# Handing the residual scaling out between feed-forward tiles and pointwise products, with no weight parts made ahead at three layer norms

## The chip, the cores and the metric

One core of a Trainium2 chip runs the whole kernel in one launch. The metric is the time of the execution on the device in microseconds; the median of several runs is what counts. The core's engines are TensorE (PE, matrix products; PEld is its loading of stationary tiles), VectorE (DVE), ScalarE (ACT) and GpSimd (POOL); the load queue on SyncE (SP) starts almost all transfers. Each engine takes its instructions strictly in order, so an instruction that waits holds up all that stand behind it on the same engine.

## The reference

Two layers of a diffusion trunk work on 256 latent and 256 context tokens of width 1024. A layer has a mixing half (attention, a convolution branch and a pooling branch, merged by gates and projected by `w_out`) and a feed-forward half. Each half ends in a residual sum and a layer norm; the context tokens are carried through the first layer only. Cut to what matters here:

```python
for l in range(DEPTH):
    ml = ada_mod(c, w_ada[l], b_ada[l], N_MOD)[:, None]
    mc = ada_mod(c_ctx, w_ada[l], b_ada[l], 2 if last else N_MOD)
    hl = modulate(x, ml[..., 0, :], ml[..., 1, :])
    ...
    x = layer_norm(DEEPNORM_ALPHA * x + ml[..., 2, :] * mix(zl, attn_l), ln1_g[l], ln1_b[l])
    x = layer_norm(DEEPNORM_ALPHA * x + ml[..., 5, :] * ffn(modulate(x, ml[..., 3, :], ml[..., 4, :])),
                   ln2_g[l], ln2_b[l])
    ...                                    # the same for ctx, in the first layer

def conv_ffn(h, w_up, dw_w, dw_b, w_down):
    a, u = jnp.split(h @ w_up, 2, axis=-1)
    a = depthwise_conv(a, dw_w, dw_b)
    return (jax.nn.silu(a) * u) @ w_down
```

So a layer norm's result goes two ways: modulated into the next product, and, scaled by the norm's gain and ALPHA, into the next residual sum. The second use isn't due until that next sum.

## The kernel before

**Products.** A float32 product is made of three: an operand is split into a rounded part hi and a remainder lo (activations into `hh` and `hl`), and PE adds hi·hi, lo·hi and hi·lo (L423, L424, L425). Results lie in four PSUM tiles `mm`; a new product needs a free one, so it waits until DVE or ACT has read the tile before it.

**Weights.** `ORDER` lists all weight chunks (128x1024, 512 KB) in the order of their use. `load_to` issues their loads on SP's queue some chunks ahead of use; chunks land in five `raw` and three `rawt` buffers. `split_to` makes a chunk's hi on ACT (L279) and its lo on DVE (L283); there are five buffers of each. `take` hands a chunk out and splits three chunks further on (L292). `take_ada` (L304) goes through the chunks of the conditioning row ("ada"), which `ada` (L340) multiplies with the conditioning vector; for a gate it adds a bias row `bg`, which is loaded at the fifth of the eight chunks (L344), into `adarow` (L356), and sends the row through DRAM to be broadcast. The layer-1 convolution's weights are split during layer 0's feed-forward half, and of these only hi is made at use.

**Residual.** `evict` multiplies a finished sum with its gate (`tg`, L540), adds the residual tile `x` (L541) and takes the statistics (L544). `norm` makes mean and inverse deviation and normalizes two 128x512 tiles, one on DVE (L559), one on ACT (L560). `modulated` transposes the result in PE (L568) and makes for each of eight slices k `hh` on ACT (L583), a float32 `h` on DVE (L585) and `hl` on DVE (L588). `scaled` multiplies each residual tile with ALPHA and the gain (L595) and adds the bias (L596): two DVE instructions a tile, eight tiles in layer 0 and four in layer 1. The gain and bias rows `prow` are loaded just before (L334).

**The order around a layer norm.** After each norm the first three weight items of the next half run slice by slice over all three (`mm_by_k`), so that PE can start with slice 0. In layer 0's first norm (L1150 to L1158) the second half of the tokens follows; then at L1169 to L1172 the bias is multiplied with ALPHA and the eight tiles are scaled, and only then the feed-forward loop (L1178) begins, which for each of 22 tiles j runs two products `pa` and `pu`, a three-tap convolution over `pa` into `acc` (ACT L1182, DVE L1186 and L1189: the last reader of `pa`), a silu (L1193), the product with `pu` (L1194) and a split for the down product (L1200, L1201). In layer 1 the scaling for the mixing half's sum stands at L1137 to L1141, behind the eight pointwise products `pw` (L1111 to L1123), where the bias of `w_out` times the gate is also joined into the bias row (L1139, L1140).

The kernel is recorded through a layer that orders each engine's instructions by their dependencies and by program order; `pin` and `keep_in_program_order` fix some of them.

## Time and profile before

| | before |
|---|---|
| median of 3 runs | 1432.54 us (1432.14 to 1434.34) |
| the profiled execution | 1433.01 us, of which the span is 1431.2 us |
| mean granted TensorE clock | 0.988 |
| PE, DVE, ACT, POOL busy | 1382.7, 1093.3, 683.0, 66.1 us |
| transfers | 265.22 MB, 185 GB/s in the mean |

A row of a list of instructions reads: start in us from the span's beginning, duration, engine, line, operation, written tile <- read tiles, shape, how many were merged; in brackets the engine's idle time ahead of it and what ended it. The granted clock is TensorE's, as a share of full speed.

The time in layer 0's first norm lies at 530 to 590 us, its second norm at 905 to 946 us; layer 1's pointwise products, `w_out`, and first norm at 1167 to 1245 us.

### The profile page before, as it was taken

What the parts mean: (1) busy time and instruction counts of PE and PEld (TensorE: products, weight loads), DVE (VectorE), ACT (ScalarE), POOL (GpSimd) and SP (SyncE); (2) the same over time, 40 slices, a digit from 0 to 9 for tenths busy, and PEclk for the clock granted to TensorE, in tenths of its full rate; (3) what the DMA queues carried; (4) which work ended last, traced back from release to release, by engine and by line L of the source; (5) the groups of instructions that cost most, each with busy time, mean ns of one, the idle gap of its engine ahead of it and who ended that gap; (6) DMA issues with size and microseconds to landing.
All of it is one profiled execution on the core that took longest, in us unless ns stands there. A gap on an engine that the chain in (4) does not pass through costs nothing.

```text
span 1431.2 us, 20768 instructions
## 1 busy us (share of the span) xinstructions
PE 1382.7 (97%) x7896; PEld 1173.4 (82%) x7896; DVE 1093.3 (76%) x1931; ACT 683.0 (48%) x1088; POOL 66.1 (5%) x65
## 2 busy tenths in 40 slices
PE   7999999999999999899999999899999999799997
PEld 5777778888877888688888888699889998799985
DVE  3598896996994778867666877378899969777745
ACT  3332446555737314445454322253687773455541
POOL 0020320000000000000000000010400000000000
PEclk9999999999999999999999999989999999899999
DMA  9654332223233526476676787588633347755560
GB/s 352 240 186 138 126 99 88 82 97 105 93 118 133 178 73 239 149 271 246 233 244 238 238 321 253 204 308 325 234 115 113 113 166 246 253 189 180 187 211 30
DMA packets 80788, 265.22 MB, mean 185 GB/s; under 512 B 9240, under 2 KB 9904, under 8 KB 80560
## 3 DMA queue, kind: packets, MB, share of 16 engines
q1 hardware_dynamic: 79968, 263.03, 52.8%
q8 instruction: 62, 1.02, 0.3%
q10 hardware_dynamic: 720, 0.87, 0.2%
...
## 4 chain that ended last, share of the span: by engine, by line
PE 88%; DVE 7%; DMA 2%; ACT 1%; issue 1%; POOL 1%; SPq 0%; POOLq 0%; DVEq 0%; ACTq 0%
PE mm L423 26%; PE mm L424 26%; PE mm L425 26%; PE ax L457 3%; DVE lo L283 1%; PE ax L991 1%; PE ad L349 1%; DVE H L780 1%; DMA prow<-in_rows 1%; PE ax L425 1%; PE ax L423 1%; PE ad L671 1%; PE ax L424 1%; DMA bg<-in_bgate 1%; DVE x L596 1%
## 5 line engine op out<-in xcount | busy, mean ns | idle before, releaser
L423 PE MATMUL mm<-hh,hi 128*128 128x256 f32 (+1 forms) x1112 | 354.6, 321 | 14.9 <-DVE acc L1189 9.8
L279 ACT ACTIVATE hi<-raw 128x1024 fp32r<-128x1024 f32 x208 | 215.8, 1046 | 309.4 <-PE mm L424 124.3
L424 PE MATMUL mm<-hl,hi 128*128 128x256 f32 (+1 forms) x1112 | 354.6, 319 | 1.6 <-DVE hl L588 1.6
L425 PE MATMUL mm<-hh,lo 128*128 128x256 f32 (+1 forms) x1112 | 354.4, 319 | 0.0
L283 DVE TENSOR_TENSOR lo<-raw,hi 128x1024 fp32r<-128x1024 f32 (+1 forms) x191 | 229.6, 1204 | 100.5 <-ACT hi L279 96.8
L780 DVE SCALAR_TENSOR_TENSOR H<-gl,vt,H 128x502 f32<-128x502 f32 (+29 forms) x480 | 264.7, 606 | 0.2
L423 PEld LDWEIGHTS mm<-hh,hi 128*128 128x128 f32 x1112 | 215.1, 194 | 30.7 <-issue 12.0
L424 PEld LDWEIGHTS mm<-hl,hi 128*128 128x128 f32 x1112 | 215.6, 194 | 16.2 <-DVE hl L588 2.4
L425 PEld LDWEIGHTS mm<-hh,lo 128*128 128x128 f32 x1112 | 215.5, 194 | 14.9 <-issue 2.0
L423 PE MATMUL mm<-hi,hi 128*128 128x512 f32 x464 | 185.2, 399 | 2.0 <-DVE nat L915 2.0
L425 PE MATMUL mm<-hi,lo 128*128 128x512 f32 x368 | 144.3, 392 | 1.1 <-DVE lo L283 1.1
L424 PE MATMUL mm<-xlo,hi 128*128 128x512 f32 x368 | 144.1, 392 | 0.0
L279 ACT ACTIVATE hi<-rawt 128x1024 fp32r<-128x1024 f32 (+1 forms) x83 | 86.7, 1048 | 108.4 <-PE mm L425 51.4
L283 DVE TENSOR_TENSOR lo<-rawt,hi 128x1024 fp32r<-128x1024 f32 (+1 forms) x72 | 86.5, 1205 | 32.5 <-ACT hi L279 32.5
L423 PEld LDWEIGHTS mm<-hi,hi 128*128 128x128 f32 x464 | 87.3, 188 | 27.7 <-issue 6.0
L423 PE MATMUL mm<-hi,ah 128*128 128x512 f32 x264 | 102.8, 390 | 0.0
L424 PE MATMUL mm<-lo,ah 128*128 128x512 f32 x264 | 102.8, 389 | 0.0
L425 PE MATMUL mm<-hi,al 128*128 128x512 f32 x264 | 102.6, 389 | 0.0
L425 PEld LDWEIGHTS mm<-hi,lo 128*128 128x128 f32 x368 | 69.1, 188 | 16.1 <-DVE lo L283 1.6
L424 PEld LDWEIGHTS mm<-xlo,hi 128*128 128x128 f32 x368 | 69.2, 188 | 13.8 <-issue 0.4
L381 DVE CUSTOM_DVE_ANT_0 prod<-rawt,cb,vt 128x1024 f32<-128x1024 f32 x48 | 61.5, 1282 | 4.2 <-DMA rawt<-in_wst 3.6
L423 PEld LDWEIGHTS mm<-hi,ah 128*128 128x128 f32 x264 | 49.6, 188 | 10.9 <-issue 0.3
...
## 6 DMA issues: line engine op xcount, KB each, us to landing
raw<-in_wst SPq DMA_DIRECT2D x232, 512.0 KB, 4.4
rawt<-in_wst SPq DMA_DIRECT2D x160, 512.0 KB, 4.3
scr<-rawt SPq DMA_DIRECT2D x28, 512.0 KB, 4.7
lo<-scr SPq DMA_DIRECT2D x28, 512.0 KB, 4.4
...
```

Of the source, the lines that this page charges most:

```text
L279: pin(A.activation(hi[:, :w], r[:, :w], AF.Copy))
L283: pin(V.tensor_tensor(lo[:, :w], r[:, :w], hi[:, :w].bitcast(F32), op=ALU.subtract))
L349: PE.matmul(ps[32 * j:32 * j + 32, :], sc[:, k, :], w[:, j * 256:(j + 1) * 256], start=(k == 0), stop=(k == KT - 1),)
L381: tc.keep_in_program_order(V.tensor_tensor_reduce(prod, w, cb[:, s], 1.0, col(l, "b_ada", m * 8 + c), ALU.mult, ALU.add, mods[l, m][:, c, ...
L423: pin(PE.matmul(ps, lh, rh, start=(first and i == 0), stop=False))
L424: pin(PE.matmul(ps, lh, rl, start=False, stop=False))
L425: pin(PE.matmul(ps, ll, rh, start=False, stop=(last and i == n - 1)))
L457: PE.matmul(ps, x[:, a:b], y[:, c:d], start=(i == 0), stop=(i == n - 1))
L596: V.tensor_tensor(x, x, b[h], op=ALU.add)
L671: pin(PE.matmul(ad0_ps[q][32 * j:32 * j + 32, :P], sc[:, k, :], w[:, j * P:(j + 1) * P], start=(k == 0), stop=(k == KT - 1),))
L780: V.scalar_tensor_tensor(h[:, :, a:b], g[:, :, a + d:b + d], col(l, "dw_w", k * 8 + j), h[:, :, a:b], op0=ALU.mult, op1=ALU.add,)
L991: PE.transpose(t_ps[:, kt * 256 + q2 * P:kt * 256 + (q2 + 1) * P], p[:, o:o + P], ID)
```

## The change

Four edits:

1. `scaled` returns a list of closures, one for each residual tile (two DVE instructions each, kept in program order) in place of doing the work. In the feed-forward loop one closure is called in each tile from j = 2 on: first the two multiplications of the bias with ALPHA, then the eight (layer 1: four) tiles.
2. In layer 1 the gate tile and the rows for the mixing half are loaded ahead of the pointwise products; at the fourth of the eight products the two bias rows are joined, and at each of the next four a residual tile is scaled.
3. A list `only` is filled at layer 0's two norms and layer 1's first: while it holds something, `take` splits only the chunk that it hands out, and `take_ada` doesn't split at all. `split_on`, called after `modulated`, ends this and splits the three chunks ahead.
4. A gate's bias row `bg` is loaded ahead of its first ada chunk, in `load_to`.

```diff
--- before.py
+++ after.py
@@ -219,8 +219,10 @@
 
 
     raw, split = {}, {}
+    bias_of = {}
     xr = []
     nxt = {"load": 0, "split": 0, "use": 0}
+    only = []
 
     others = [i for i, it in enumerate(ORDER) if it[0] not in ("ada", "adt", "pre", "ad0", "x")]
     sides = [i for i, it in enumerate(ORDER) if it[0] in ("adt", "pre")]
@@ -247,6 +249,9 @@
                 continue
             if it[0] == "pre":
                 w = CH
+            if it[0] == "ada" and it[3] == 0 and it[1:3] in GATES:
+                bias_of[it[1:3]] = S(name="bg")
+                load(bias_of[it[1:3]][:, :256], bgate[GATES.index(it[1:3])], False)
 
             if it[0] in ("adt", "pre") or (not side(nxt["load"]) and nxt["load"] % (NRAW + NRAWT) >= NRAW):
                 t = wp.tile([P, CH], F32, tag="rawt", name=f"rawt{nxt['load']}", bufs=NRAWT)
@@ -289,7 +294,7 @@
             i = nxt["use"]
             nxt["use"] += 1
             load_to(i + (LA0 if strict else LA))
-            split_to(i if strict else ahead[i])
+            split_to(i if strict or only else ahead[i])
             if ORDER[i][0] not in ("ada", "adt", "pre") and unfinished:
                 unfinished[0][0] -= 1
                 if not unfinished[0][0]:
@@ -307,7 +312,6 @@
             i = nxt["use"]
             nxt["use"] += 1
             load_to(i + LA)
-            split_to(ahead[i])
             if ORDER[i][0] == "ada":
                 ada(*ORDER[i][1:])
             else:
@@ -315,13 +319,17 @@
         while unfinished:
             unfinished.pop(0)[1]()
 
+    def split_on():
+        only.clear()
+        split_to(ahead[nxt["use"] - 1])
+
 
     sc = const.tile([P, KT, 32], F32, name="sc")
     V.memset(sc, 0.0)
     A.activation(sc[:, :, 0:2], ct, AF.Silu)
     mods = {}
     ada_ps = {}
-    gate_row, bias_of = {}, {}
+    gate_row = {}
 
     def row_tiles(src, name):
 
@@ -341,9 +349,6 @@
         w = raw.pop(("ada", l, m, k))
         if k == 0:
             ada_ps[l, m] = pad.tile([P, 256], F32, tag="ad", name=uid("ad"))
-        if k == 4 and (l, m) in GATES:
-            bias_of[l, m] = S(name="bg")
-            load(bias_of[l, m][:, :256], bgate[GATES.index((l, m))], False)
         ps = ada_ps[l, m]
         for j in range(4):
             PE.matmul(
@@ -589,11 +594,12 @@
 
         def scaled(self, tts, g, b):
 
-            for tt in tts:
-                for h in range(2):
-                    x = self.res[tt][h]
-                    V.scalar_tensor_tensor(x, x, ALPHA, g[h], op0=ALU.mult, op1=ALU.mult)
-                    V.tensor_tensor(x, x, b[h], op=ALU.add)
+
+            def one(x, h):
+                tc.keep_in_program_order(V.scalar_tensor_tensor(x, x, ALPHA, g[h], op0=ALU.mult, op1=ALU.mult))
+                tc.keep_in_program_order(V.tensor_tensor(x, x, b[h], op=ALU.add))
+
+            return [lambda x=self.res[tt][h], h=h: one(x, h) for tt in tts for h in range(2)]
 
     def affine(l, name, shift, scale, tag):
 
@@ -1110,6 +1116,10 @@
             xres = [[], [], [], []]
         its = [(take(("pw", l, c)), mmb()) for c in range(GRP)]
         mm_by_k(its, cT_, range(KT), T)
+        todo = []
+        if l == 1:
+            gates, ob = gate_tiles(l, 2), param_row(l, 0)
+            g, b = param_row(0, 3), param_row(0, 4)
         for c in range(8):
             ps = its[c][1] if c < GRP else mmB(take(("pw", l, c)), cT_, T)
             if l == 0:
@@ -1121,11 +1131,18 @@
             )
             madd(c, t)
             mT.append(hilo(mt[c], T, "m"))
+            if l == 1 and c == GRP:
+                for h in range(2):
+                    V.tensor_tensor(ob[h], gates[0][h], ob[h], op=ALU.mult)
+                    V.scalar_tensor_tensor(b[h], b[h], ALPHA, ob[h], op0=ALU.mult, op1=ALU.add)
+                todo = r.scaled((0, 1), g, b)
+            elif todo:
+                todo.pop(0)()
         mixctx.close()
 
 
-        gates, ob = gate_tiles(l, 2), param_row(l, 0)
         if l == 0:
+            gates, ob = gate_tiles(l, 2), param_row(l, 0)
             for s in range(2):
                 for h in range(2):
                     t = S(name="gb")
@@ -1134,11 +1151,7 @@
                         x = xres[tt][h]
                         V.scalar_tensor_tensor(x, x, ALPHA, t, op0=ALU.mult, op1=ALU.add)
         else:
-            g, b = param_row(0, 3), param_row(0, 4)
-            for h in range(2):
-                V.tensor_tensor(ob[h], gates[0][h], ob[h], op=ALU.mult)
-                V.scalar_tensor_tensor(b[h], b[h], ALPHA, ob[h], op0=ALU.mult, op1=ALU.add)
-            r.scaled((0, 1), g, b)
+            assert not todo
         while unfinished:
             unfinished.pop(0)[1]()
         aff = affine(l, "ln1", mods[l, 3], mods[l, 4], f"m{l}")
@@ -1148,6 +1161,7 @@
         if ns == 2:
 
             token_products(l, "wout", mT, r, lambda: None, None)
+            only.append(1)
             r.modulated(0, *aff, hs, T)
             ws = [take(("up", l, j, h)) for j, h in up]
             take_ada()
@@ -1155,21 +1169,23 @@
             hT2 = [hs[k] for k in range(KT)]
             mm_by_k(its, hT2, range(KT), T, 0)
             r.modulated(1, *aff, hs, T)
+            split_on()
             mm_by_k(its, hT2, range(KT), T, 1)
         else:
             token_products(l, "wout", mT, r, None, r.norm)
+            only.append(1)
             ws = [take(("up", l, j, h)) for j, h in up]
             take_ada()
             r.modulated(0, *aff, hs, T)
+            split_on()
             hT2 = [hs[k] for k in range(KT)]
             its = [(w, mmb()) for w in ws]
             mm_by_k(its, hT2, range(KT), T)
         upps = {x: ps for x, (_, ps) in zip(up, its)}
 
         g, b = param_row(l, 1), param_row(l, 2)
-        for h in range(2):
-            V.tensor_scalar(b[h], b[h], ALPHA, None, op0=ALU.mult)
-        r.scaled(range(nt), g, b)
+        todo = [lambda h=h: V.tensor_scalar(b[h], b[h], ALPHA, None, op0=ALU.mult) for h in range(2)]
+        todo += r.scaled(range(nt), g, b)
 
 
         ffctx = ExitStack()
@@ -1190,6 +1206,8 @@
                 a3[:, :, :-1], p3[:, :, 1:], col(l, "fdw_w", 2 * FT + j), a3[:, :, :-1], op0=ALU.mult, op1=ALU.add,
             )
             run_due(1)
+            if j >= 2 and todo:
+                todo.pop(0)()
             A.activation(acc[:, :T], acc[:, :T], AF.Silu)
             V.tensor_tensor(acc[:, :T], acc[:, :T], pu[:, :T], op=ALU.mult)
             if j < NFF and not last:
@@ -1214,11 +1232,13 @@
             run_due(len(due))
             aff = affine(l, "ln2", mods[1, 0], mods[1, 1], "n")
             convpre = {}
+            only.append(1)
             for j in range(GRP):
                 it = ("conv", 1, j // 2, j % 2)
                 convpre[it] = take(it), None
             take_ada()
             r.modulated(0, *aff, hs, NTOK)
+            split_on()
             hT = [hs[k] for k in range(KT)]
             later.append(lambda r=r, aff=aff, hs=hs: r.modulated(1, *aff, hs, NTOK))
         else:
```

How that moves instructions, at three places. Numbers behind a name are the program's tile numbers; lines in rows of the changed kernel are its own (L599 and L600 are `scaled`, L1202 and L1205 the two taps into `acc`, L288 the remainder of a weight chunk, L1187 the bias times ALPHA).

The first is DVE in layer 0 between the first norm and the feed-forward loop. Before, the last twelve of the rows that begin with the scaling and end with the last reader of the first `pa`, `mm775`:

```order
L595 SCALAR_TENSOR_TENSOR x675_4373<-x675_4373,prow787_5249 128x512
L595 SCALAR_TENSOR_TENSOR x680_4413<-x680_4413,prow786_5247 128x512
L596 TENSOR_TENSOR x675_4373<-x675_4373,prow789_5253 128x512
L596 TENSOR_TENSOR x680_4413<-x680_4413,prow788_5251 128x512
L595 SCALAR_TENSOR_TENSOR x685_4453<-x685_4453,prow787_5249 128x512
L595 SCALAR_TENSOR_TENSOR x691_4501<-x691_4501,prow786_5247 128x512
L596 TENSOR_TENSOR x685_4453<-x685_4453,prow789_5253 128x512
L596 TENSOR_TENSOR x691_4501<-x691_4501,prow788_5251 128x512
L595 SCALAR_TENSOR_TENSOR x696_4541<-x696_4541,prow787_5249 128x512
L1186 SCALAR_TENSOR_TENSOR acc790_5276<-mm775_5052,vt0_82,acc790_5276 128x2x255
L596 TENSOR_TENSOR x696_4541<-x696_4541,prow789_5253 128x512
L1189 SCALAR_TENSOR_TENSOR acc790_5276<-mm775_5052,vt0_82,acc790_5276 128x2x255
```

and now, from the last `hl` of the norm on:

```order
L593 TENSOR_TENSOR hl771_4976<-h32785_5157,hh770_4975 128x256
L1187 TENSOR_SCALAR prow788_5251<-prow788_5251 128x512
L288 TENSOR_TENSOR lo159_5172<-raw159_5011,hi159_5171 128x1024
L1202 SCALAR_TENSOR_TENSOR acc790_5258<-mm775_5040,vt0_82,acc790_5258 128x2x255
L288 TENSOR_TENSOR lo161_5271<-raw161_5023,hi161_5270 128x1024
L1205 SCALAR_TENSOR_TENSOR acc790_5258<-mm775_5040,vt0_82,acc790_5258 128x2x255
L1202 SCALAR_TENSOR_TENSOR acc794_5299<-mm777_5042,vt0_82,acc794_5299 128x2x255
```

The sixteen instructions of the eight residual tiles are no longer between `hl` and `acc`; two remainders and one row product are. The feed-forward loop of layer 1 begins in the same way: there four tiles and both row products went from ahead of the first `acc`.

The second is ACT at layer 0's second norm, where the chunks 289 and 290 belong to the first items of layer 1's convolution. Before:

```order
L560 ACTIVATE x696_4541<-x696_4541,nm992_7829,lrs991_7826 128x512
L279 ACTIVATE hi289_7847<-raw289_7845 128x1024
L279 ACTIVATE hi290_7853<-raw290_7851 128x1024
L583 ACTIVATE hh998_7917<-ax997_7912,sBn_7834,sAn_7833 128x256
L583 ACTIVATE hh1001_7923<-ax997_7912,sBn_7834,sAn_7833 128x256
L583 ACTIVATE hh1004_7933<-ax1003_7928,sBn_7834,sAn_7833 128x256
```

and now:

```order
L565 ACTIVATE x696_4541<-x696_4541,nm993_7831,lrs992_7828 128x512
L588 ACTIVATE hh998_7905<-ax997_7900,sBn_7836,sAn_7835 128x256
L284 ACTIVATE hi289_7964<-raw289_7847 128x1024
L588 ACTIVATE hh1001_7911<-ax997_7900,sBn_7836,sAn_7835 128x256
L284 ACTIVATE hi290_7968<-raw290_7854 128x1024
L588 ACTIVATE hh1004_7921<-ax1003_7916,sBn_7836,sAn_7835 128x256
```

The first `hh` stands ahead of both chunks now, and the second ahead of chunk 290.

The third is DVE at the end of layer 1's pointwise products, the last two of which (`mm1413`, `mm1417`) are read into the halves of `pwo1414`. Now:

```order
L600 TENSOR_TENSOR x662_4309<-x662_4309,prow1399_11059 128x512
L1129 SCALAR_TENSOR_TENSOR pwo1414_11228<-mm1413_11203,vt1_83,g11368_10847 128x256
L439 TENSOR_TENSOR mlo1411_11156<-m1260_10030,mhi1410_11154 128x256
L599 SCALAR_TENSOR_TENSOR x666_4318<-x666_4318,prow1398_11057 128x512
L1023 TENSOR_TENSOR m1347_10561<-m1347_10561,pwo1414_11228 128x256
L600 TENSOR_TENSOR x666_4318<-x666_4318,prow1400_11061 128x512
L439 TENSOR_TENSOR mlo1416_11233<-m1347_10561,mhi1415_11231 128x256
L599 SCALAR_TENSOR_TENSOR x670_4327<-x670_4327,prow1397_11055 128x512
L288 TENSOR_TENSOR lo360_11240<-raw360_10968,hi360_11239 128x1024
L600 TENSOR_TENSOR x670_4327<-x670_4327,prow1399_11059 128x512
L1129 SCALAR_TENSOR_TENSOR pwo1414_11228<-mm1417_11243,vt1_83,g11368_10847 128x256
L288 TENSOR_TENSOR lo361_11288<-raw361_11081,hi361_11287 128x1024
```

Before, the corresponding operations stood behind the last `mlo`:

```order
L434 TENSOR_TENSOR mlo1408_11209<-m1347_10561,mhi1407_11207 128x256
L1139 TENSOR_TENSOR prow1412_11251<-gate1410_11247,prow1412_11251 128x512
L1139 TENSOR_TENSOR prow1413_11253<-gate1411_11249,prow1413_11253 128x512
L595 SCALAR_TENSOR_TENSOR x662_4309<-x662_4309,prow1414_11255 128x512
L595 SCALAR_TENSOR_TENSOR x666_4318<-x666_4318,prow1415_11257 128x512
L595 SCALAR_TENSOR_TENSOR x670_4327<-x670_4327,prow1414_11255 128x512
L1140 SCALAR_TENSOR_TENSOR prow1416_11259<-prow1416_11259,prow1412_11251 128x512
L1140 SCALAR_TENSOR_TENSOR prow1417_11261<-prow1417_11261,prow1413_11253 128x512
L596 TENSOR_TENSOR x662_4309<-x662_4309,prow1416_11259 128x512
L596 TENSOR_TENSOR x666_4318<-x666_4318,prow1417_11261 128x512
L596 TENSOR_TENSOR x670_4327<-x670_4327,prow1416_11259 128x512
```

What moved is eight instructions of `scaled` and four on the bias rows, to between the readers of the products; the reader of the last product, `mm1417`, stands behind six of the eight and behind the remainder of chunk 360.

## The prediction

> **What bounds the kernel now.** I read the busy shares first, then the chain of work that ended last, then PE's waits, then the stretches around the longest of them.
>
> ```profile
> PE 1382.7 (97%) x7896; PEld 1173.4 (82%) x7896; DVE 1093.3 (76%) x1931; ACT 683.0 (48%) x1088; POOL 66.1 (5%) x65
> ...
> DVE  3598896996994778867666877378899969777745
> ...
> PE 88%; DVE 7%; DMA 2%; ACT 1%; issue 1%; POOL 1%; SPq 0%; POOLq 0%; DVEq 0%; ACTq 0%
> ...
> PE mm L423 <- DVE acc L1189: 9.8, 2, 6.4
> ...
> PE mm L423 <- ACT hh L583: 5.1, 2, 4.5
> ...
> PE ax L568 <- DVE x L559: 2.2, 1, 2.2
> ...
> PE mm L424 <- DVE hl L588: 1.6, 2, 0.9
> ...
> PE mm L424 <- DVE lo L283: 0.8, 1, 0.8
> ```
>
> PE is busy nearly always and carries 88% of the chain: only time in which PE waits, or runs at a lower clock, can be won. The rows of waits (total, times, longest, us) name what this change touches: 9.8 + 5.1 + 2.2 + 1.6 + 0.8 = 19.5 us, 1.4% of the span. Busy PE time at a low clock comes on top and is in no row of waits; the windows by stage show it.
>
> **Part A, layer 0's first norm.** Eight residual tiles are scaled between the norm and the first feed-forward tile.
>
> ```profile
> 566.43 1.90 DVE L595 SCALAR_TENSOR_TENSOR x<-x,prow 128x512 f32<-128x512 f32 x3 [1.82 <-DMA prow<-in_rows]
> 568.24 0.42 DVE L1171 TENSOR_SCALAR prow<-prow 128x512 f32<-128x512 f32 x1
> 568.58 1.22 DVE L283 TENSOR_TENSOR lo<-raw,hi 128x1024 fp32r<-128x1024 f32 x1
> ...
> 578.53 0.74 DVE L1189 SCALAR_TENSOR_TENSOR acc<-mm,vt,acc 128x510 f32<-128x510 f32 x1
> ...
> 569.60 0.77 ACT L1182 ACTIVATE acc<-mm,vt 128x512 f32<-128x512 f32 x1
> ...
> 579.42 0.76 PE L423 MATMUL mm<-hh,hi 128*128 128x512 f32 x1 [6.41 <-DVE acc L1189]
> ...
> 580.00:585.00 5.00, 5.00 (x17) 3.99 (x16) 5.00 (x7) 1.26 (x2) 0.00 (x0) 0.67 0.55 166
> ...
> 582.74 0.43 PE mm L424
> ...
> 583.75 0.23 PE mm L424
> ```
>
> PE's last free PSUM tile is used up at 573.01 (579.42 - 6.41). The first to come free is the first `pa`, once L1189 has read it at 579.2; DVE does that after its sixteen instructions. Then PE starts cold: in the window (length; PE, PEld, DVE, ACT, POOL busy; clock; DMA) the clock is 0.67, and a product is 0.43 us until it becomes 0.23 at 583.5. From 579.4 to 583.5 that is 9.5 products at 0.2 us too much, 1.9 us.
>
> Now DVE has the bias product, a remainder, L1186, a remainder, L1189. The bias row was there at 568.24. From then, by the durations above, 0.42 + 1.22 + 0.74 + 1.22 + 0.74 ends at 572.6, 0.4 us before PE asks. ACT's two `acc`, done by 570.4, don't hold it. So 6.4 us of wait go, and with them the cold start: **8.3 us**. Bounds: 5, if loading of the bias row or a remainder comes 3 us later, and 8.4. The sixteen instructions (1.90 us for three, so 10 us) go to j = 4 to 11, 1.3 us a tile. A tile gives PE 48 products of 0.23 us, 11 us; in the page's slices of 35.8 us that hold the loop, the 17th to 23rd, DVE is busy six to eight tenths, so there is room of 2 us or more a tile. That is the cover, and without it up to 10 us would come back.
>
> **Part B, layer 0's second norm.**
>
> ```profile
> 925.68 1.06 ACT L279 ACTIVATE hi<-raw 128x1024 fp32r<-128x1024 f32 x1 [2.39 <-DMA raw<-in_wst]
> 926.96 1.06 ACT L279 ACTIVATE hi<-raw 128x1024 fp32r<-128x1024 f32 x1 [0.22 <-DMA raw<-in_wst]
> 927.92 0.55 ACT L583 ACTIVATE hh<-ax,sBn,sAn 128x256 fp32r<-128x256 f32 x1
> ...
> 928.52 1.23 PE L423 MATMUL mm<-hh,hi 128*128 128x256 f32 x4 [4.52 <-ACT hh L583]
> ...
> 932.38 0.42 DVE L356 TENSOR_TENSOR adarow<-ad,bg 128x256 f32<-128x256 f32 x1 [2.16 <-DMA bg<-in_bgate]
> 932.73 0.41 DVE L588 TENSOR_TENSOR hl<-h,hh 128x256 fp32r<-128x256 f32 x1
> 933.06 0.54 DVE L585 TENSOR_SCALAR h<-ax,sAn,sBn 128x256 f32<-128x256 f32 x1
> ...
> 922.54 0.60 PE ax L568 x4
> ...
> 930.00:935.00 5.00, 4.08 (x19) 3.79 (x19) 2.60 (x7) 1.12 (x3) 0.00 (x0) 0.50 1.01 389
> ...
> 937.83 0.21 PE mm L423
> ...
> 938.92 0.12 PE mm L424
> ...
> 945.88 1.31 PE ax L568 x12
> ```
>
> The transposes that the first `hh` reads are done at 923.1, but two splits stand ahead of it on ACT, and both wait for their chunk. PE idles 4.52 us; then DVE waits for the gate's bias row, whose load was issued only at the fifth ada chunk; and from 928.5 to 938.3 a product takes 0.21 us in place of 0.12. The next half's transposes come at 945.88.
>
> Now, with the same landings: first `hh` 923.3 to 923.9, PE's first slice 924.0 to 925.8. The second `hh` stands behind chunk 289 (925.68 + 1.06): 926.8 to 927.3; PE waits 1.6 us for it and about 0.5 for its `hl`. The third stands behind chunk 290: to 928.9, its `hl` at 929.9. From there DVE makes one slice in 1.1 us (0.54 + 0.42, and what lies between), PE nine products of 0.12: both 1.1 us. The eighth slice ends at 929.9 + 5 x 1.1 + 0.7 = 936.1, the 24 products of the fourth item at 939.0. **6.9 us** saved. DVE has nothing between its last `hl` and the first convolution item, so the taps that follow move up as well; no row of PE's waits names a cause in that convolution, so I take it that the gain is kept. Bounds: 3 (below) and 7.7 (if PE doesn't wait for the third slice).
>
> **Part C, layer 1's pointwise products to the feed-forward loop.**
>
> ```profile
> 1195.59 1.22 DVE L283 TENSOR_TENSOR lo<-raw,hi 128x1024 fp32r<-128x1024 f32 x1 [1.30 <-ACT hi L279]
> ...
> 1200.12 1.29 DVE L595 SCALAR_TENSOR_TENSOR x<-x,prow 128x512 f32<-128x512 f32 x2 [0.83 <-DMA prow<-in_rows]
> ...
> 1222.01 2.18 PE L568 MATMUL ax<-ID,x 128*128 128x128 f32 x9 [2.22 <-DVE x L559]
> ...
> 1238.27 1.22 DVE L283 TENSOR_TENSOR lo<-raw,hi 128x1024 fp32r<-128x1024 f32 x1 [2.11 <-ACT hi L279]
> ...
> 1244.10 0.36 PE L423 MATMUL mm<-hh,hi 128*128 128x256 f32 x1 [3.41 <-DVE acc L1189]
> ...
> 1185.00:1190.00 5.00, 5.00 (x44) 5.00 (x43) 5.00 (x9) 2.62 (x4) 0.00 (x0) 1.00 0.75 252
> ...
> 1245.00:1250.00 5.00, 5.00 (x32) 5.00 (x31) 3.80 (x7) 2.15 (x4) 0.00 (x0) 0.66 0.65 210
> ```
>
> At the feed-forward loop's start the mechanism is that of A. A remainder ends at 1239.5 (1238.27 + 1.22); L1186, a second remainder and L1189 add 0.5 + 1.2 + 0.5 (an estimate for the readers, which are half as wide as A's of 0.74 us): released at about 1241.7 where it was 1244.0. PE asked at 1240.7. Of 3.41 us of wait some 1.0 is left: 2.4 us. The clock of 0.66 from 1245 to 1250 is that of some 3.3 us at half speed, 1.6 us too much; with 1.0 us idle I count that as gone. Together 4.0.
>
> Against it: DVE is full from 1185 to 1190, and twelve instructions of about 0.6 us, 7.2 us, now go in between the readers of the pointwise products. PE has four PSUM tiles, and I expect it to wait 1 to 3 us for one, or for chunk 360's remainder, around the change to `w_out`. In return DVE's two idle pieces of 1.30 and 0.83 us fill up, it reaches `evict` up to 2.1 us sooner, the 0.8 us wait for a remainder goes, and the norm, which DVE ends last (2.22 us of PE's waiting), comes sooner. The price has the window's 7.2 us as its worst end and nothing as its best; the four free tiles make me take 2 us, the return 2.4. **C: 4.0 + 0.4 = 4.4 us**, bounds 0 and 6.
>
> **Small edits.** The other three bias rows, 128 KB each, come sooner on SP's queue. Nothing: they are small beside the 512 KB chunks. Loads of row tiles in layer 1 start sooner, with a tile of a shared pool held longer: nothing, since loads there wait for chunks' buffers and not for these; if a chunk is held back, at most the 4.4 us that one takes to land.
>
> ```profile
> raw<-in_wst SPq DMA_DIRECT2D x232, 512.0 KB, 4.4
> ```
>
> **The sum.** 8.3 + 6.9 + 4.4 = 19.6 us from the profiled execution's 1433.0 us: 1413.4 us. The median of 1432.54 differs from that execution by 0.5 us, a fiftieth of the sum, and I let it be.
>
> **Where the clock rule matters.** The clock stayed at 1.00 through one wait and fell after another that is hardly longer:
>
> ```profile
> 1167.50 0.74 PE L423 MATMUL mm<-ch,hi 128*128 128x256 f32 x4 [1.96 <-ACT ch L1099]
> ...
> 1165.00:1170.00 5.00, 2.86 (x22) 2.42 (x21) 2.32 (x4) 4.97 (x10) 0.00 (x0) 1.00 0.52 187
> ...
> 1225.00:1230.00 5.00, 4.31 (x19) 4.02 (x20) 4.54 (x10) 2.04 (x4) 0.00 (x0) 0.50 0.97 366
> ```
>
> At 1222.01 only 2.22 us of idle time, with shorter pieces around it, led to 0.50. Part B's remaining waits (1.6 us, 0.5, 0.9) lie between these two cases. The Trainium skill, page "TensorE: Matmul & The Clock Gate", section "Part 1: The HAM clock gate (the "warmup" mystery)", says that a whole idle window of about 3.4 us halves the clock and that the windows run free. By that rule no wait left in part B would halve it, and B would be worth 6.9 us; the row at 1222.01 disagrees, since 2.22 us did, and by it B would be worth 3.6.
>
> **The rivals.**
> - *The clock falls at the second norm all the same.* Nine products a slice take 1.9 us and not 1.1 for four slices, 3.3 us more; and C's pointwise wait comes out at 3 us in place of 2, or the cold start in C stays at 1.6. For it: 1222.01. Against it: 1167.50. Time: 1413.4 + 3.3 + 1.3 = 1418.
> - *B's gain is taken back in the convolution.* The weights for its first items must come 7 us sooner while transfers are at a share of 1.01 (930 to 935). For it: ACT waits twice for a chunk at 925.68 and 926.96. Against it: an item of 24 products of 0.23 us uses one 512 KB chunk in 5.4 us, under 100 GB/s of the 389 in that window. Time: 1413.4 + 6.9 = 1420.
> - *Weights come late after the norms, slower than before.* Three chunks are split after each of three norms and not before; a split is 1.06 on ACT and 1.22 on DVE, 2.3 us in a row. If none lies beside PE's work, PE waits 6.8 us at each norm, 20.5 us in all, which uses up the 19.6, and a cold start of 1.9 us at each makes 5.7 more: 1433.0 + 0.9 + 5.7 = 1440. It decides from the point at which the first of them starts less than 2.3 us before PE has finished the slices. Against it: that PE has 24 products of the fourth item there, or 72 of the first three, 2.9 to 8.6 us, and in A the remainders fit in the sum above.
> - *The change doesn't do what it says*: the handed out scaling gathers on DVE and PE waits in the loop instead. It would give A's and C's waits back, 8.3 + 4.4: 1426, and with B gone too no change. The order shown speaks against it.
>
> **How the numbers follow.** Forecast 0.58 (1413.4), clock falls 0.22 (1418), taken back 0.09 (1420), gathered waits 0.06 (half of it 1426, half no change), weights late 0.05 (half of it slower by over 0.2%, half within or a little faster). The predicted time is the likeliest's. The range goes from the upper bounds of A and B with C at its own upper end, 1433.0 - 22.1 = 1411, less 3 us for waits between stages that I can't see, to 1425: the lower bounds' sum is 5 + 3 + 0 = 8. Outside lie the gathered waits and the late weights, about 1 in 10. About 0.2%, 2.9 us, is what a measurement of this kernel can tell from no change. Faster by over that 0.93, within 0.04, slower 0.03.
>
> **What would show it.** In the changed profile: no wait of PE for `acc` at layer 0's loop, clock 1.00 in all windows there (A). PE's wait for the first `hh` at the second norm under 1 us, no DVE wait for `bg`, transposes of the second half about 7 us sooner; the clock there tells the first rival (B). In C a wait of PE of 1 to 3 us between the fifth pointwise product and the first slices of `w_out`, and about 1 us for `acc` at the loop. Wrong I would be if PE waited for `lo` or `hi` in the first items after a norm, or for chunks in the convolution.

## The result and the profile after

| | before | changed |
|---|---|---|
| median of 4 runs each | 1432.65 us (1432.14 to 1434.34) | 1413.78 us (1411.37 to 1416.13) |
| the profiled execution | 1433.01 us, span 1431.2 us | 1416.13 us, span 1414.3 us |
| mean granted TensorE clock in it | 0.988 | 0.995 |

The ratio is 0.9864, 95% interval 0.985 to 0.9879: the changed kernel is faster, and 1413.4 us was predicted. The profiled execution is the slowest of the four, 2.35 us above their median; what follows is read from it. On the page, PE's row, with busy time and share of the span first:

```profile
PE 1377.6 (97%) x7896; PEld 1168.2 (83%) x7896; DVE 1093.9 (77%) x1931; ACT 683.1 (48%) x1088; POOL 66.2 (5%) x65
```

Five microseconds of busy time are gone with the same 7896 instructions: that is time at a low clock. The rest was idle. Of PE's waits (total, times, longest) these answer to the ones shown of before:

```profile
PE mm L429 <- DVE hl L593: 2.4, 2, 2.0
...
PE mm L428 <- ACT hh L588: 1.4, 2, 0.8
...
PE ax L573 <- DVE x L564: 1.1, 1, 1.1
PE mm L428 <- DVE gl L810: 0.9, 2, 0.7
PE mm L428 <- DVE acc L1205: 0.9, 1, 0.9
...
PE mm L429 <- DVE lo L288: 0.7, 1, 0.7
...
PE ax L495 <- DVE H L786: 0.4, 1, 0.4
PE mm L428 <- DVE pwo L1129: 0.3, 1, 0.3
```

The wait for `acc` went from 9.8 to 0.9 us, that for `hh` from 5.1 to 1.4. New are `gl` and `H`, tiles of layer 1's convolution, and `pwo`, the reader of the pointwise products.

To see where in the program the time went, I took the start of the same PE instruction in both traces at stage borders, and compare the lengths of the stages between them:

| stage | before, us | changed, us less (-) or more |
|---|---|---|
| start to the last `q` product (192.5) | 192.53 | -0.37 |
| to the first score (210.4) | 17.83 | +1.36 |
| to the last `w_out` product of layer 0 (539.9) | 329.55 | -0.02 |
| A: to the last down product of layer 0 (918.6) | 378.66 | -8.48 |
| B, norm: to the transposes of the second half (945.7) | 27.14 | -7.20 |
| B, convolution: to the first `kv` products (982.5) | 36.79 | +2.87 |
| to the rotation's transposes (1015.4) | 32.90 | -0.68 |
| to the channel norm's products `ch` (1167.5) | 152.10 | +0.10 |
| C, pointwise products: to `w_out` (1191.5) | 24.0 | +2.12 |
| C, `w_out` (1214.5) | 23.0 | -0.42 |
| C, norm (1224.7) | 10.3 | -2.01 |
| C, feed-forward loop to the down product (1360.8) | 136.0 | -3.99 |

The sum is -16.72 us. Stage A, list of instructions on DVE (start, duration):

```profile
565.22 0.42 DVE L1187 TENSOR_SCALAR prow<-prow 128x512 f32<-128x512 f32 x1
568.86 1.23 DVE L288 TENSOR_TENSOR lo<-raw,hi 128x1024 fp32r<-128x1024 f32 x1 [3.22 <-ACT hi L284]
570.00 0.74 DVE L1202 SCALAR_TENSOR_TENSOR acc<-mm,vt,acc 128x510 f32<-128x510 f32 x1
570.66 1.22 DVE L288 TENSOR_TENSOR lo<-raw,hi 128x1024 fp32r<-128x1024 f32 x1
571.79 0.74 DVE L1205 SCALAR_TENSOR_TENSOR acc<-mm,vt,acc 128x510 f32<-128x510 f32 x1
```

The last reader of the first `pa` ends at 572.5, where it was 579.2. PE never waits for `acc` there, and the clock stays full, as in this window (length; PE, PEld, DVE, ACT, POOL busy, with the number of instructions; clock; DMA share and GB/s):

```profile
570.00:575.00 5.00, 5.00 (x24) 4.14 (x23) 5.00 (x8) 3.79 (x6) 0.00 (x0) 1.00 0.64 199
```

Stage B, the second norm of layer 0, first ACT and then PE:

```profile
916.43 0.56 ACT L588 ACTIVATE hh<-ax,sBn,sAn 128x256 fp32r<-128x256 f32 x1 [0.64 <-PE ax L573]
918.35 1.06 ACT L284 ACTIVATE hi<-raw 128x1024 fp32r<-128x1024 f32 x1 [1.35 <-DMA raw<-in_wst]
919.31 0.55 ACT L588 ACTIVATE hh<-ax,sBn,sAn 128x256 fp32r<-128x256 f32 x1
...
918.09 0.39 PE L429 MATMUL mm<-hl,hi 128*128 128x256 f32 x1 [0.41 <-DVE hl L593]
...
919.91 0.73 PE L428 MATMUL mm<-hh,hi 128*128 128x256 f32 x4 [0.84 <-ACT hh L588]
```

The first `hh` is made as soon as its transposes are there; PE's 4.52 us of waiting for it are gone, and the longest wait that is left there is 0.84 us for the second `hh`, behind a chunk that came from memory at 918.3. The three stretches of the table from the last down product to the rotation, in before and then in the changed kernel, show what became of the gain:

```profile
918.57:945.71 27.14, 21.70 (x178) 19.04 (x177) 11.59 (x26) 10.97 (x16) 0.54 (x1) 0.81 0.79 288
945.71:982.50 36.79, 36.70 (x307) 36.50 (x306) 34.47 (x85) 19.86 (x29) 3.74 (x4) 1.00 0.99 367
982.50:1015.40 32.90, 32.90 (x148) 27.13 (x147) 30.18 (x78) 14.17 (x34) 4.47 (x4) 1.00 0.80 298
```

```profile
911.06:931.00 19.94, 18.12 (x179) 15.34 (x177) 11.32 (x25) 9.69 (x14) 0.54 (x1) 1.00 0.83 309
931.00:970.66 39.66, 38.14 (x312) 37.20 (x311) 35.72 (x86) 21.10 (x31) 3.56 (x4) 1.00 1.02 385
970.66:1002.88 32.22, 32.22 (x144) 26.61 (x143) 29.61 (x76) 13.94 (x34) 4.47 (x4) 1.00 0.67 254
```

In the norm PE's idle time falls from 5.44 to 1.82 us (27.14 - 21.70; 19.94 - 18.12) and the clock rises from 0.81 to 1.00. In the convolution it rises from 0.09 to 1.52 us. DVE is busy there for 35.7 of 39.7 us, as it was before for 34.5 of 36.8. Five more PE instructions stand ahead of the `kv` products now (312 for 307), four of them transposes of `H`, which came behind them before; so 0.68 us of the 2.87 come back in the next stretch. Net, B is worth 27.14 + 36.79 + 32.90 less 19.94 + 39.66 + 32.22: 5.01 us.

Stage C, PE's list of instructions, and the windows behind the first and the fourth of the rows:

```profile
1155.08 0.74 PE L428 MATMUL mm<-ch,hi 128*128 128x256 f32 x4 [1.96 <-ACT ch L1105]
...
1169.58 0.39 PE L428 MATMUL mm<-ch,hi 128*128 128x256 f32 x1 [0.34 <-DVE pwo L1129]
...
1210.22 1.21 PE L573 MATMUL ax<-ID,x 128*128 128x128 f32 x9 [1.07 <-DVE x L564]
...
1214.74 0.44 PE L429 MATMUL mm<-hl,hi 128*128 128x256 f32 x1 [1.99 <-DVE hl L593]
...
1228.88 0.36 PE L428 MATMUL mm<-hh,hi 128*128 128x256 f32 x1 [0.88 <-DVE acc L1205]
```

```profile
1155.00:1160.00 5.00, 4.74 (x26) 4.54 (x27) 2.13 (x5) 5.00 (x13) 0.00 (x0) 0.69 0.92 238
...
1215.00:1220.00 5.00, 5.00 (x31) 5.00 (x31) 5.00 (x13) 2.60 (x5) 0.00 (x0) 0.66 0.92 343
```

The wait for `ch` of 1.96 us is that of before, to the hundredth; but there the clock stayed at 1.00 behind it, and here it fell to 0.69. The 1.36 us lost ahead of the first score, a part of the program that the change doesn't touch, are of the same kind. The wait for `qTlo` in before, and then in the changed kernel, each with its window:

```profile
202.05 0.66 PE L906 MATMUL ax<-ID,rot 128*128 128x128 f32 x4 [2.78 <-DVE qTlo L434]
...
200.00:205.00 5.00, 2.95 (x24) 2.21 (x25) 4.73 (x10) 3.79 (x9) 2.25 (x2) 1.00 0.30 108
```

```profile
201.67 1.11 PE L912 MATMUL ax<-ID,rot 128*128 128x128 f32 x4 [2.77 <-DVE qTlo L439]
...
200.00:205.00 5.00, 3.33 (x15) 2.92 (x15) 3.69 (x8) 2.72 (x6) 1.88 (x2) 0.66 0.35 108
```

### The profile page after: what moved, and what is told of

Read it like the earlier page. It is cut to its first block, busy times and chain, and to the rows that moved or that the text cites. A ratio compares the mean times of both kernels' runs of the same rounds, so it can differ in the third digit from the quotient of the medians.

```text
span 1414.3 us, 20776 instructions
## 1 busy us (share of the span) xinstructions
PE 1377.6 (97%) x7896; PEld 1168.2 (83%) x7896; DVE 1093.9 (77%) x1931; ACT 683.1 (48%) x1088; POOL 66.2 (5%) x65
## 3 DMA queue, kind: packets, MB, share of 16 engines
q8 instruction: 62, 1.02, 0.3%
## 4 chain that ended last, share of the span: by engine, by line
PE 81%; DVE 7%; issue 6%; DMA 2%; POOL 2%; ACT 2%; SPq 0%; POOLq 0%; ACTq 0%; DVEq 0%
PE mm L428 24%; PE mm L429 24%; PE mm L430 24%; PE ax L462 3%; DVE H L786 2%; DVE lo L288 1%; PE ax L997 1%; PE ad L354 1%; POOL gc L827 1%; DMA raw<-in_wst 1%; PE ax L428 1%; PE ax L430 1%; PE ax L429 1%; PE ad L677 1%; DMA lo<-scr 0%
## 5 line engine op out<-in xcount | busy, mean ns | idle before, releaser
L429 PE MATMUL mm<-hl,hi 128*128 128x256 f32 (+1 forms) x1112 | 349.9, 316 | 2.4 <-DVE hl L593 2.4
L428 PE MATMUL mm<-hh,hi 128*128 128x256 f32 (+1 forms) x1112 | 348.8, 317 | 3.2 <-ACT hh L588 1.4
L430 PE MATMUL mm<-hh,lo 128*128 128x256 f32 (+1 forms) x1112 | 350.4, 316 | 0.0
L288 DVE TENSOR_TENSOR lo<-raw,hi 128x1024 fp32r<-128x1024 f32 (+1 forms) x191 | 229.9, 1206 | 104.2 <-ACT hi L284 100.3
L786 DVE SCALAR_TENSOR_TENSOR H<-gl,vt,H 128x502 f32<-128x502 f32 (+29 forms) x480 | 265.8, 612 | 0.2
L429 PEld LDWEIGHTS mm<-hl,hi 128*128 128x128 f32 x1112 | 212.4, 191 | 16.6 <-DVE hl L593 3.0
L428 PEld LDWEIGHTS mm<-hh,hi 128*128 128x128 f32 x1112 | 210.5, 191 | 18.7 <-ACT hh L588 1.9
L430 PEld LDWEIGHTS mm<-hh,lo 128*128 128x128 f32 x1112 | 212.4, 191 | 14.8 <-issue 2.0
L288 DVE TENSOR_TENSOR lo<-rawt,hi 128x1024 fp32r<-128x1024 f32 (+1 forms) x72 | 86.8, 1208 | 31.9 <-ACT hi L284 31.9
```

What stands on the lines that cost most here:

```text
L288: pin(V.tensor_tensor(lo[:, :w], r[:, :w], hi[:, :w].bitcast(F32), op=ALU.subtract))
L428: pin(PE.matmul(ps, lh, rh, start=(first and i == 0), stop=False))
L429: pin(PE.matmul(ps, lh, rl, start=False, stop=False))
L430: pin(PE.matmul(ps, ll, rh, start=False, stop=(last and i == n - 1)))
L786: V.scalar_tensor_tensor(h[:, :, a:b], g[:, :, a + d:b + d], col(l, "dw_w", k * 8 + j), h[:, :, a:b], op0=ALU.mult, op1=ALU.add,)
```

## The experiments

Three questions: which edit brings what; whether A needs the handing out at all; and what takes part of B and C back. The stages A, B and C below are those of the table, from one profiled execution each: B from the last down product to the rotation (96.83 us in before), C from `ch` to the end of the feed-forward loop (193.24 us in before). The four kernels that left B's code alone had B between -2.05 and +0.99 us against before, so a difference of up to 3 us there means nothing by itself. The clock is behind it: at the second norm it stayed at 0.50 for 10.24 us in before, e1_ff and f4_busy, and for 3.41 us in e3_pw and f1_pinned, after waits of 4.1 to 4.8 us in all five. PE's waits are the safer measure of what an edit does there.

### One part at a time

Each of four kernels is the kernel before with one part of the change.

**e1_ff**: edit 1 alone. At the pointwise products the scaling stays where it was.

```diff
+            for f in r.scaled((0, 1), g, b):
+                f()
...
+        todo = [lambda h=h: V.tensor_scalar(b[h], b[h], ALPHA, None, op0=ALU.mult) for h in range(2)]
+        todo += r.scaled(range(nt), g, b)
...
+            if j >= 2 and todo:
+                todo.pop(0)()
```

> The kernel before with only the scaling of the two feed-forward loops handed out (edit 1); layer 1's scaling at the pointwise products stays behind them, the parts ahead and the bias rows are as before. Theory (each edit works at its own place): 8.5 us less at layer 0's first norm (6.4 us of PE's wait for acc and the cold start behind it), nothing at the second norm, where PE still waits 4.5 us for the first hh, and about 4 us less at layer 1's loop: 1420 us. Rival (the handed out scaling wins only because no parts are made ahead, since the remainders stand ahead of acc on DVE in either case): half of it, 1426 us.

**e2_norms**: edits 3 and 4 alone.

```diff
+                bias_of[it[1:3]] = S(name="bg")
+                load(bias_of[it[1:3]][:, :256], bgate[GATES.index(it[1:3])], False)
...
-            split_to(i if strict else ahead[i])
+            split_to(i if strict or only else ahead[i])
...
-            split_to(ahead[i])
...
+            only.append(1)
...
+            split_on()
```

> The kernel before with only edits 3 and 4 (no parts ahead at the three norms, bias rows early); all scaling is done in place. Theory: 7 us less up to the second half's transposes of layer 0's second norm, of which 2 us are given back in the convolution that follows, since DVE works on its taps without a gap there; nothing at layer 0's loop (the 6.4 us wait for acc stays) and at most 1 us in layer 1: 1427 us. Rival (what is given back in the convolution is the weights' transfers, saturated there): PE waits there for hi, lo or a chunk and not for gl or H, and 4 us or more are given back.

**e3_pw**: edit 2 alone. The scaling ahead of the feed-forward loop isn't handed out, but its pairs are kept in program order, since both places use the same `scaled`.

```diff
+            if l == 1 and c == GRP:
...
+                todo = r.scaled((0, 1), g, b)
+            elif todo:
+                todo.pop(0)()
...
-        r.scaled(range(nt), g, b)
+        for f in r.scaled(range(nt), g, b):
+            f()
```

> The kernel before with only layer 1's scaling handed out at the pointwise products (edit 2). Theory: PE loses 0.3 us at the products (a wait for pwo) and, if the clock falls after its wait for ch there, 1.7 us more; DVE reaches the last evict 1 to 2 us sooner; the 3.4 us wait for acc at layer 1's loop stays: 1431 to 1433 us, not to be told from before. Rival (the twelve instructions among the readers of the products cost PE 2 us, as was predicted): PE waits 1 us or more for pwo or for lo between the fifth product and w_out's first slices, with the clock at 1.00.

**e4_bias**: edit 4 alone (the first two added lines of e2_norms, in place of the load at the fifth chunk).

> The kernel before with only the bias rows loaded early (edit 4). Theory (the first hh behind two splits is what costs at layer 0's second norm): DVE's wait of 2.2 us for the bias row goes and with it PE's 0.9 us wait for hl, the 4.5 us wait for the first hh and the half clock stay: 1 to 2 us less, 1431 us. Rival (the late bias row is what keeps PE slow there): 4 us or more less up to the second half's transposes.

| | median, us | ratio to before (1433.87) | A | B | C |
|---|---|---|---|---|---|
| e1_ff | 1418.27 | 0.9887 [0.9869, 0.9905] | -8.47 | +0.99 | -5.68 |
| e2_norms | 1428.55 | 0.9964 [0.9951, 0.9977] | -0.38 | -3.03 | -0.80 |
| e3_pw | 1421.79 | 0.9924 [0.9909, 0.9939] | -8.07 | -1.75 | -2.23 |
| e4_bias | 1427.54 | 0.9955 [0.9936, 0.9974] | -0.11 | -3.27 | -2.06 |

e1_ff bears the theory out; A and C together are worth 14.2 us in its profile. e3_pw missed its expectation by some 10 us: A comes though nothing is handed out at layer 0's loop. What that loop has of the edit is the pinning of the pairs, which f1_pinned tries by itself. In e4_bias one row's load brings as much as edits 3 and 4 bring together, which I had given to edit 3: PE's wait at the norm is 1.79 us, and 1.82 in e2_norms, where before has 4.52. Its ACT rows have the order of the changed kernel, though no splitting was put off:

```profile
924.55 0.57 ACT L584 ACTIVATE hh<-ax,sBn,sAn 128x256 fp32r<-128x256 f32 x1 [0.17 <-PE ax L569]
927.40 1.06 ACT L283 ACTIVATE hi<-raw 128x1024 fp32r<-128x1024 f32 x1 [2.29 <-DMA raw<-in_wst]
928.37 0.55 ACT L584 ACTIVATE hh<-ax,sBn,sAn 128x256 fp32r<-128x256 f32 x1
```

Its norm stage is 5.30 us shorter and its convolution 2.71 us longer. That of e2_norms is 5.19 shorter, 2.85 longer: the gain is given back in the same place without edits 1 and 2.

### Where the readers of acc stand; what the taps and the bias row do; busy waits

**f1_pinned**: the kernel before, nothing handed out; only the pairs of `scaled` are kept in program order.

```diff
+            def one(x, h):
+                tc.keep_in_program_order(V.scalar_tensor_tensor(x, x, ALPHA, g[h], op0=ALU.mult, op1=ALU.mult))
+                tc.keep_in_program_order(V.tensor_tensor(x, x, b[h], op=ALU.add))
...
-        r.scaled(range(nt), g, b)
+        for f in r.scaled(range(nt), g, b):
+            f()
```

> The kernel before; scaled still does all its work in place, but each pair of its two DVE instructions is now kept in program order, as in the changed kernel's closures. The edit moves them on DVE: the two readers of acc now stand behind one and two pairs and not behind sixteen instructions. Theory (what PE waits for is only where the two readers of the first pa stand on DVE, wherever the rest of the scaling goes): PE's 6.4 us wait at layer 0's loop falls to 1 us or less and the cold start goes, 8 us less there; in layer 1 the wait of 3.4 us falls to about 2: 1423 us. Rival (it is the handing out over the tiles that wins, since DVE has as much work between the norm and the second tile as before): PE's wait at layer 0's loop stays above 4 us.

Measured: 1420.76 us (1419.82 to 1424.51) against 1433.93, ratio 0.9914 [0.9883, 0.9945]; A -7.93, C -2.96. DVE's list:

```profile
569.74 0.68 DVE L594 SCALAR_TENSOR_TENSOR x<-x,prow 128x512 f32<-128x512 f32 x1
570.34 0.74 DVE L1189 SCALAR_TENSOR_TENSOR acc<-mm,vt,acc 128x510 f32<-128x510 f32 x1
571.00 0.68 DVE L595 TENSOR_TENSOR x<-x,prow 128x512 f32<-128x512 f32 x1
571.60 0.69 DVE L594 SCALAR_TENSOR_TENSOR x<-x,prow 128x512 f32<-128x512 f32 x1
572.20 0.74 DVE L1192 SCALAR_TENSOR_TENSOR acc<-mm,vt,acc 128x510 f32<-128x510 f32 x1
```

Pinning one pair behind the other keeps the scaling from gathering ahead of `acc`: the two readers stand behind one and three of the sixteen instructions, the other thirteen come after them among the loop's own instructions, and PE waits 0.30 us for the second. So A turns on the place of `acc`'s readers on DVE; handing out adds 0.5 us (e1_ff). In layer 1's loop pinning alone does less: a wait of 2.58 us for `acc` is left, with a low clock behind it, and the stage from the norm to the down product is 2.67 us shorter than in before. With handing out (e1_ff) the wait is 1.23 us, the clock stays full behind it, and the stage is 5.25 us shorter.

**f2_late_bias**: the changed kernel without edit 4.

```diff
-            if it[0] == "ada" and it[3] == 0 and it[1:3] in GATES:
-                bias_of[it[1:3]] = S(name="bg")
-                load(bias_of[it[1:3]][:, :256], bgate[GATES.index(it[1:3])], False)
...
+        if k == 4 and (l, m) in GATES:
+            bias_of[l, m] = S(name="bg")
+            load(bias_of[l, m][:, :256], bgate[GATES.index((l, m))], False)
```

> The changed kernel with its bias rows loaded at the fifth ada chunk again (edit 4 undone). Theory (the early bias row is what frees the norm's start, and no parts ahead adds little): at layer 0's second norm the first hh stands behind a split again and hl behind the bias row; PE waits 3 us or more for hh, the clock falls, and 4 to 6 us are lost up to the second half's transposes, of which 2 are made good in the convolution: 1417 us. Rival (edit 3 carries the second norm): no more than 1.5 us lost there.

Measured: 1416.43 us (1414.54 to 1416.82), 0.9873 [0.9849, 0.9897]; B -4.83 where the changed kernel has -5.01. PE waits 2.17 us for the second `hh` in place of 0.84, the clock stays at 1.00, and the rotation begins within 0.14 us of the changed kernel's. The theory expected 3 us or more of wait and a lower clock, so its rival holds. Edits 1 and 2 leave PE's wait at 4.6 to 4.8 us (e1_ff, e3_pw). So edit 3 brings the gain here without edit 4, and edit 4 does in e4_bias without edit 3; together they bring no more that these profiles can tell.

**f3_taps**: the changed kernel with DVE's taps of layer 1's convolution (`H`, L786) kept out of that stretch; they are done later, and none is left out.

```diff
-NTAPS = ((10, 6, 10, 1000), (12, 7, 11, 1000))
+NTAPS = ((10, 6, 10, 1000), (0, 9, 12, 1000))
```

> The changed kernel with layer 1's convolution taps handed out only after the last convolution item (the first of the four counts that say how many taps follow an item is 0 in place of 12). Theory (the 2 to 3 us given back in that convolution are PE's waits for gl, which stands on DVE behind 13 to 16 taps): no wait of PE for gl or H between the second norm and the key product, which then comes 2 to 3 us sooner after the norm than in the changed kernel; later the taps are missing time before the pointwise products, where PE waits longer. Rival (transfers or the slower pace of the merged products): the same time from the norm to the key product, within 0.5 us.

Measured in a single run: 1456.97 us, since the taps now hold PE up later (13.5 us for `H`). What the run was for are B's stretches:

```profile
910.85:930.25 19.40, 17.93 (x178) 15.44 (x177) 11.23 (x25) 9.58 (x14) 0.54 (x1) 1.00 0.85 316
930.25:967.25 37.00, 36.94 (x309) 36.68 (x307) 9.93 (x23) 20.79 (x30) 2.84 (x4) 1.00 1.02 399
```

With DVE at 9.9 us of 37.0, PE's idle time in the convolution is 0.06 us where it was 1.52, while transfers move as much as before the edit (share 1.02 in both). The stretch is 0.2 us longer than in before (37.00 against 36.79), where the changed kernel's is 2.87 longer. PE's waits there come from DVE's taps, which stand ahead of `gl` and `H`; they don't come from transfers.

**f4_busy**: the kernel before, with transposes that nothing reads filling PE's two waits for `acc`.

```diff
+    def busy(n):
+        t = aux()
+        for _ in range(n):
+            tc.keep_in_program_order(PE.transpose(t[:, :P], ID, ID))
...
+            if j == 2:
+                busy(26 if l else 50)
```

> The kernel before with transposes that nobody reads put into PE's two waits for acc at the loops: 50 of them (5.9 us) in layer 0, 26 (3.0 us) in layer 1. Nothing that is waited for comes sooner. Theory (the slow products behind the waits come from PE's idleness alone): the granted clock stays at 1.00 behind both, layer 0's loop comes 1.9 us sooner and layer 1's 1.6: 1430 us. Rival (the clock falls for another reason, the load on the other engines or the restart itself): 0.50 behind the waits as before, no gain.

Measured: 1430.34 us (1426.02 to 1432.42), 0.9967 [0.9952, 0.9981]; A -2.03. PE's list, a window that lies within the transposes, and the one behind them:

```profile
573.97 5.62 PE L418 MATMUL ax<-ID 128*128 128x128 f32 x50
580.34 0.47 PE L428 MATMUL mm<-hh,hi 128*128 128x512 f32 x1 [0.76 <-DVE acc L1196]
...
573.63:577.04 3.41, 3.41 (x32) 3.28 (x31) 3.41 (x7) 1.06 (x1) 0.00 (x0) 1.00 0.00 0
580.00:585.00 5.00, 4.66 (x21) 3.88 (x22) 5.00 (x8) 1.26 (x2) 0.00 (x0) 1.00 0.39 116
```

The product that waited starts no sooner; but the clock behind it is 1.00 and not 0.67, and 2.0 us are saved. The cold start was put at 1.9.

### The price of edit 2, and the cold starts left

**g0_changed** is the changed kernel again, for its spread.

> The changed kernel once more, for a fair comparison with the two kernels beside it. Expected 1411 to 1417 us, and at its two waits of fixed length ahead of layer 0's scores (2.8 us) and layer 1's pointwise products (2.0 us) the granted clock now at 1.00 and now at 0.50.

**g1_warm**: the changed kernel with such transposes in the waits of layer 1.

```diff
+                if T == SEQ and i == 3:
+                    busy(16, pad.tile([P, 256], F32, tag="ad", name=uid("ad")))
...
+            if l == 1 and i == 2:
+                busy(15, aux())
...
+            busy(8, aux())
```

> The changed kernel with transposes that nobody reads in three of PE's waits in layer 1: 15 ahead of the last transposes before the pointwise products (the 2.0 us wait for ch), 8 behind the ada products of the first norm and 16 ahead of that norm's first products (waits of 1.1 and 2.0 us). Theory (a low clock comes from PE's idleness, and these waits cost cold products behind them): the clock stays at 1.00 from the pointwise products to the feed-forward loop, 1.5 to 2 us less at the norm, and 0 or 1.7 us less at the products, which had their cold start in half of the profiles: 1411 us, about 2.5 us below the changed kernel. Rival (DVE sets the end of the norm anyway, so that a faster PE waits longer): the clock at 1.00 and less than 0.7 us less.

**g2_no_pw**: the changed kernel with edit 2 undone; the scaling stands behind the pointwise products again, in pairs.

```diff
-            if l == 1 and c == GRP:
...
-                todo = r.scaled((0, 1), g, b)
-            elif todo:
-                todo.pop(0)()
...
+            for f in r.scaled((0, 1), g, b):
+                f()
```

> The changed kernel with layer 1's scaling for the mixing half back behind the pointwise products (edit 2 undone; its pairs still in program order). Theory (the handing out at the products saves and costs little): from the first pointwise product to the loop's end within 1 us of the changed kernel in a profile with the same clock there, 1414 us. Rival (as was predicted, it costs PE 2 us at the products and saves DVE 2 us at the norm): 2 us sooner at w_out's start, 2 us later at the norm.

**h1_best**: g2_no_pw with the transposes of g1_warm, and twelve more behind the first slice of the second norm of layer 0.

```diff
+            mm_by_k(convpre.values(), hT, range(1), T)
+            busy(12, pad.tile([P, 256], F32, tag="ad", name=uid("ad")))
+            mm_by_k(convpre.values(), hT, range(1, KT), T)
```

> The changed kernel with the pointwise-products part undone (pairs kept in program order) and with products whose result nothing reads put into TensorE's waits at the second norm of layer 0 (12), the last chunk transposes (15), behind the adapter (8) and at the first norm of layer 1 (16). Theory (the losses left in layer 1 and at the second norm are cold starts after waits of 1.5 to 2.4 us, not missing data): clock 1.00 in the microseconds behind each of these waits, the stretch from the first channel transposes to the end of the last feed-forward 7 us shorter than before, and a median of 1410 to 1411 us. Rival (DVE's chain sets the ends there, so a warm TensorE only waits longer): the waits grow by what the clock saves and the median is within 1 us of 1413.4. A third way: the unread products delay the products behind them, 1415 us or more.

| | median, us | ratio to before | C, pointwise products | C |
|---|---|---|---|---|
| changed | 1413.78 | 0.9864 [0.985, 0.9879] | +2.12 | -4.30 |
| g0_changed | 1414.46 | 0.9872 [0.9858, 0.9887] | +0.60 | -4.60 |
| g1_warm | 1413.22 | 0.9859 [0.9842, 0.9875] | +0.60 | -6.98 |
| g2_no_pw | 1413.58 | 0.9863 [0.9846, 0.9879] | +0.01 | -7.39 |
| h1_best | 1412.19 | 0.9856 [0.984, 0.9873] | 0.00 | -7.61 |

The clock stayed at 1.00 behind the `ch` wait in g0_changed, and edit 2's price there was 0.60 us. With unread products in the waits (g1_warm, h1_best) it is full all through C, where g0_changed has 10.2 us at 0.50, from 1209.1 to 1219.3. C is 2.4 us shorter in g1_warm than in g0_changed: so much did the transposes bring there. The median is only 1.2 us lower and not the 1411 us of the theory, and the two intervals overlap. g2_no_pw shows that edit 2 brings nothing that can be measured: without it C is -7.39 us in a profile with one short cold start there, and the two medians lie 0.2 us apart. h1_best has full clock behind every wait it fills and C at -7.61, as its theory had it; its median is the lowest, but lies 1.2 us above what that theory gave, and its interval overlaps the others. It isn't shown to be faster than the changed kernel.

## Why the prediction was right, and where not

**Part A: right.** 8.3 us forecast, 8.48 measured. The last reader of the first `pa` ended at 572.5; 572.6 was worked out from row durations. The handed out instructions cost nothing in the loop: PE waits nowhere there for `acc` in layer 0. The prediction gave this to the handing out. f1_pinned shows that less is enough: with the scaling left in the program where it was, but in pinned pairs, 7.93 of the 8.48 us come as well.

**Part B: the size at the norm came out, the step after it was wrong.** At the norm 6.9 us were forecast and 7.20 came. That they agree so well is partly luck: e3_pw and f1_pinned, with the code of before at this place and less time at the low clock, are 1.74 and 2.05 us shorter there than before, and against them the changed kernel's norm gains 5.2 to 5.5 us. The second `hh` was ready 8.8 us into the stage (919.31 + 0.55 - 911.06), and 8.7 was forecast (927.3 - 918.57), so the landings were as assumed. PE's waits were smaller, 0.41 and 0.84 us against 1.6, 0.5 and some 0.9, because its first slice came 0.6 us later than forecast and its last transposes lay between the slices. The step that failed is "no row of PE's waits names a cause in that convolution, so I take it that the gain is kept". Of the 7.20 us 2.19 went again (2.87 less 0.68), and B is worth 5.01. 1.43 us of that is PE's new idle time (1.52 against 0.09), of which the rows of waits give 0.9 to `gl` and 0.4 to `H`; the other 0.76 us are PE busy time on what is but for one instruction the same work. f3_taps shows DVE's taps as the cause of both: without them in that stretch PE's idle time is 0.06 us, its busy time 36.94 where before has 36.70, and B is worth 8.21 us, so that nothing is given back. How a late reader lengthens PE's busy time isn't shown. That no wait stood there in before didn't mean that there was room: DVE was busy for 34.5 of 36.8 us, a number that one window of the trace of before would have given. The rival that had the gain taken back named transfers, and was wrong in that: in f3_taps they stay as full.

Nor did B need both of its edits: edit 4 brings the gain without edit 3 (e4_bias), as does edit 3 without edit 4 (f2_late_bias). How the place of one load moves ACT's order, through the layer that orders the instructions, no run took apart.

**Part C: the sum was right, in part by luck.** 4.4 us forecast, 4.30 measured: 3.99 at the loop (4.0 forecast), 2.43 back at `w_out` and the norm (2.4), 2.12 lost at the pointwise products (2). But the loss was to be a wait of 1 to 3 us for a PSUM tile or a remainder. PE waited 0.34 us for `pwo` and 0.7 for `lo` where it had waited 0.8 before; g0_changed puts the whole price at 0.60. The other 1.5 us are a cold start behind the wait for `ch`, which edit 2 doesn't touch. Nor can the return be put down to edit 2: without it, in g2_no_pw, C as a whole is larger. At the loop the mechanism is borne out, since PE waits 0.88 us for `acc` where 1.0 was forecast, and the clock stays full behind it. But the 3.99 us hold the norm's first slices too, with a low clock that varies: g0_changed, with the same wait of 0.88 us, is 2.79 us shorter there than before.

**The clock.** The rival in which it falls at the second norm all the same did not come about in the profiled execution (1.00 after 0.84 us of wait). It did in e2_norms, e4_bias, g1_warm and g2_no_pw, behind waits of 1.82, 1.79, 1.50 and 2.33 us. What that cost shows in PE's busy time on the norm's stretch, in g2_no_pw:

```profile
910.69:932.96 22.27, 19.52 (x178) 16.85 (x177) 11.24 (x25) 9.65 (x14) 0.54 (x1) 0.92 0.75 276
```

That is 1.40 us more than the 18.12 of the changed kernel, where the rival had 3.3: the low clock ended after some 3 us. The Trainium skill, page "TensorE: Matmul & The Clock Gate", section "Part 1: The HAM clock gate (the "warmup" mystery)", gives a whole idle window of about 3.4 us as what halves the clock. These four falls, and those after 1.96 us, don't agree with it: in the 3.41 us that ended with the fall PE was still busy for 0.32 to 0.50 of the time. What it says of the windows' length, and that they run free, agrees with the traces (the last section). The prediction put its waits of 1.6, 0.5 and 0.9 us "between" the two cases of 1.96 and 2.22 us; each of them is shorter than both, and the length of a single wait was the wrong measure.

**The sum.** A, B and C gave 17.79 us where 19.6 were forecast. The cold start ahead of the first score took 1.36 more in this execution. The profiled execution went from 1433.01 to 1416.13, a gain of 16.9; the medians differ by 18.9. That the median lies 0.4 us from the forecast is thus partly luck: B was 1.9 too large, and the low clock behind PE's waits, which differs from one execution to the next, moves single terms of the sum by 1 to 2 us.
